# First weights in two transfers, two tiles of x rounded by two engines, and the second tile's products by kind, at the start of a hybrid encoder layer

## The chip, the cores and the metric

The kernel runs on one core of a Trainium2 chip. A core has five engines that run at the same time, each through its own instructions in order: TensorE (PE, the matrix multiplier, with its weight loads, PEld), VectorE (DVE), ScalarE (ACT), GpSimd (POOL) and SyncE (SP, which here only issues transfers). They wait for one another by semaphores. The metric is the device time of one execution, in microseconds (us); lower is better.

## The reference

One layer of an encoder on x of 512 positions by 1024 channels, all in float32:

```
h    = RMSNorm(x) * attn_norm_g
[xr | gate | q | k | v] = h @ w_in                 # 1024 x 2560
y1   = (forward RG-LRU + backward RG-LRU of conv4(xr)) * gelu(gate)
y2   = dilated attention of q, k, v (8 heads, three windows)
x    = x + [RMSNorm(y1) | RMSNorm(y2)] @ w_out
x    = x + relu(RMSNorm(x) @ w_up)^2 @ w_down      # 1024 x 4096 x 1024
out  = RMSNorm(x) * final_norm_g
```

The RG-LRU needs, per channel, a constant softplus(-lam). Only the first line, the first 384 columns of `w_in` and this constant are touched by the change.

## The kernel before

Every large product is made of three matmuls in a rounded float32 type (`FR`): with each operand split into a rounded part `hi` and a remainder `lo`, the product is hi*hi + hi*lo + lo*hi. `mm3` (lines 302 to 305) issues the three for one weight block. The rounding to `hi` is a copy (or a copy with a scale) on ScalarE or DVE, and the remainder `lo` is a subtraction on DVE.

The order of the instructions of TensorE, ScalarE, DVE and GpSimd is the order of the program text; only SP's transfers are put in order by a scheduler, behind what frees their buffers.

The beginning, with the names that matter:

- On TensorE, eight warm-up matmuls of a tile of ones (`pwarm`, line 145) stand ahead of everything. `vt` holds the vectors of gains and constants; ScalarE's queue loads it.
- x comes transposed, in eight tiles of 128 channels by 512 positions, each with the 384 columns of `w_in` that belong to its channels behind it (`xw[k]`, 128 x 896). SP loads them (lines 324 to 327); tile 0 comes in two transfers, x and then weights.
- `cvx(k)` (lines 331 to 341) rounds a tile: `h_hi` is x times the gain, rounded, on ScalarE (333); `w3h` is the rounded weights, on DVE for tile 0 (336) and on ScalarE for the others (338); `h_lo` (339) and `w3l` (340) are the remainders, on DVE.
- `sq(k)` squares x on ScalarE (345), and `addsq` adds the squares up on DVE (348). The sum over tiles gives the RMS of each position. The norm's division comes only after the product, so the matmuls need not wait for it.
- `softplus_consts` (147 to 173) computes the constant of the RG-LRU in pieces, on tiles of 128 x 8: a call of `next(spc)` issues the piece up to the next `yield`. The first piece is two DVE operations (153, 154), the second an exponential on ScalarE (156), the third two DVE operations (158, 159) and the first part of a chain of small GpSimd operations (160 to 167).
- The product of the first 384 columns (lines 405 to 415) adds into three banks `pxr[t]`: nine matmuls a tile. For tile 0 they go by kind: three of h_hi and w3h, three of h_lo and w3h, three of h_hi and w3l. For tiles 1 to 7 each bank has its three in a row (`mm3`). Ahead of tile 7, `col_sums` (402) multiplies the sum of squares, as stationary operand, with a column of ones; then DVE (387), a power on GpSimd (390) and four transposes on TensorE (382) make the row `rrow` by which the products are scaled.

From there on, the weights stream in chunks of 128 x 1024 that `conv_hi` (249 or 251) and `conv_lo` (259) round.

Of the kernel before, what the change touches and what calls it, by code (L numbers as in the profile page):

```python
# [14 lines left out]
AF = mybir.ActivationFunctionType  # L15
OP = mybir.AluOpType

P = 128
S = 512
# [80 lines left out]
def hybrid_kernel(ctx: ExitStack, tc, xw, xn, w_in, w_v, w_out, w_up, w_dn, gates, vecs, rel, onehot, fg, out):  # L100
    nc = tc.nc
# [8 lines left out]
    act = nc.scalar.activation  # L110
# [3 lines left out]
    def g_(name, dt=FT, shape=(P, S)):  # L114
        return work.tile(list(shape), dt, name=name, tag="g", bufs=NG)
# [4 lines left out]
    def ps_(name, tag):  # L120
        return psum.tile([P, S], FT, name=name, tag=tag, bufs={"pj": 4, "gs": 2, "et": 2}[tag])

    def f(t):
        return t.bitcast(FT)
# [5 lines left out]
    def vec(n, i):  # L130
        return vt[:, VEC[n] + i:VEC[n] + i + 1]
# [15 lines left out]
    def softplus_consts():  # L147
        ts, tt = nc.gpsimd.tensor_scalar, nc.gpsimd.tensor_tensor
        lam = vt[:, VEC["lam"]:VEC["lam"] + 8]
        e8, sp, z, z2, pl = [small(n, 8) for n in ("e8", "sp8", "z8", "z28", "pl8")]  # L150
        cneg = consts.tile([P, 8], FT, name="cneg")
        chalf = consts.tile([P, 8], FT, name="chalf")
        stt(e8, lam, -1.0, lam, op0=OP.mult, op1=OP.max)
        nc.vector.tensor_scalar(sp, lam, -1.0, 0.0, op0=OP.mult, op1=OP.max)
        yield
        act(e8, e8, AF.Exp, scale=-1.0)
        yield
        nc.vector.tensor_scalar(z, e8, 2.0, None, op0=OP.add)
        nc.vector.reciprocal(z, z)
        tt(z, z, e8, op=OP.mult)  # L160
        tt(z2, z, z, op=OP.mult)
        ts(pl, z2, 1.0 / 19, 1.0 / 17, op0=OP.mult, op1=OP.add)
        for c in (15, 13, 11, 9, 7, 5, 3, 1):
            if c == 7:
                yield
            tt(pl, pl, z2, op=OP.mult)
            ts(pl, pl, 1.0 / c, None, op0=OP.add)
        tt(pl, pl, z, op=OP.mult)
        ts(pl, pl, 2.0, None, op0=OP.mult)
        tt(sp, pl, sp, op=OP.add)  # L170
        ts(cneg, sp, -LRU_C, None, op0=OP.mult)
        ts(chalf, sp, 0.5 * LRU_C, None, op0=OP.mult)
        yield cneg, chalf

    spc = softplus_consts()
    next(spc)


    chunks = []
# [122 lines left out]
    def mm3(o, a, b, first, last, on=False):  # L302
        nc.tensor.matmul(o, lhsT=a[0], rhs=b[0], start=bool(first), stop=False, skip_group_check=on)  # L303
        nc.tensor.matmul(o, lhsT=a[0], rhs=b[1], start=False, stop=False, skip_group_check=on)  # L304
        nc.tensor.matmul(o, lhsT=a[1], rhs=b[0], start=False, stop=bool(last), skip_group_check=on)  # L305
# [8 lines left out]
    h_hi = big.tile([P, KD, S], FR, name="h_hi", tag="bigA")  # L314
    h_lo = big.tile([P, KD, S], FR, name="h_lo", tag="bigB")
    XW = S + 3 * P
    xwt, w3 = [], []
    for k in range(KD):
        if 4 <= k < 7:
            xwt.append(stream.tile([P, 1024], FT, name="wraw", tag="wraw", bufs=3)[:, :XW])  # L320
        else:
            xwt.append(work.tile([P, 1024], FT, name="tw", tag="tw", bufs=4)[:, :XW])
        if k == 0:
            nc.sync.dma_start(xwt[0][:, :S], xw[0][:, :S])
            nc.sync.dma_start(xwt[0][:, S:], xw[0][:, S:])
        else:
            nc.sync.dma_start(xwt[k], xw[k])

# [1 line left out]

    def cvx(k):
        x, w = xwt[k][:, :S], xwt[k][:, S:]
        act(h_hi[:, k, :], x, AF.Copy, scale=vec("ag", k))
        hi, lo = g_("w3h", FR), g_("w3l", FR)
        if k == 0:
            nc.vector.tensor_copy(hi[:, :3 * P], w)
        else:
            act(hi[:, :3 * P], w, AF.Copy)
        stt(h_lo[:, k, :], x, vec("ag", k), f(h_hi)[:, k, :], op0=OP.mult, op1=OP.subtract)
        nc.vector.tensor_tensor(lo[:, :3 * P], w, f(hi)[:, :3 * P], op=OP.subtract)  # L340
        w3.append((hi, lo))

    def sq(k):
        sqx[k] = g_("sqx")
        act(sqx[k], xwt[k][:, :S], AF.Square)

    def addsq(k):
        nc.vector.tensor_tensor(sqx[0], sqx[0], sqx.pop(k), op=OP.add)

    cvx(0)  # L350
    next(spc)
    sq(0)
    next(spc)
    for k in range(1, KD):
        cvx(k)
        sq(k)
        if k >= 2:
            addsq(k - 1)
# [7 lines left out]
    def hk(k):  # L366
        return (h_hi[:, k, :], h_lo[:, k, :])

    def wk(c, k):
        if c < 3:  # L370
            return tuple(t[:, c * P:(c + 1) * P] for t in w3[k])
        hi, lo = splits[c]
        return (hi[:, k * P:(k + 1) * P], lo[:, k * P:(k + 1) * P])
# [11 lines left out]
    def rstd_cols(ssc, n):  # L385
        v = small("rv", 4)
        nc.vector.tensor_scalar(v, ssc, 1.0 / n, EPS, op0=OP.mult, op1=OP.add)
        r = consts.tile([P, 4], FT, name="rcol_%d" % st["rc"])
        st["rc"] += 1
        nc.gpsimd.tensor_tensor(r, v, mhalf, op=OP.pow)  # L390
        return r
# [7 lines left out]
    def col_sums(ss, tag):  # L399
        pc = ps_("pcs", tag)  # L400
        for tt in range(4):
            nc.tensor.matmul(pc[:, tt:tt + 1], lhsT=ss[:, tt * P:(tt + 1) * P], rhs=ones[:, 0:1], start=True, stop=True)
        return pc[:, 0:4]

    pxr = {t: ps_("pxr", "pj") for t in range(3)}
    for k in range(KD):
        if k == KD - 1:
            rcol = rstd_cols(col_sums(sqx[0], "et"), D)
        if k == 0:
            for i, (a, b) in enumerate(((0, 0), (0, 1), (1, 0))):  # L410
                for t in range(3):
                    nc.tensor.matmul(pxr[t], lhsT=wk(t, 0)[a], rhs=hk(0)[b], start=i == 0, stop=False)
            continue
        for t in range(3):
            mm3(pxr[t], wk(t, k), hk(k), False, k == KD - 1)
# [251 lines left out]
    for n, (k, tt) in enumerate(steps):  # L667
        c = C_V + k // 2
        if k == 0:
            pv[tt] = ps_("pv", vtag[tt])  # L670
        hi, lo = splits[c]
# [433 lines left out]
    for w in OSEQ:  # L1105
        for i in range(4):
            tt, k = (i % 2, i // 2) if w == "s2" else (i // 2, i % 2)
# [239 lines left out]
    for half in range(2):  # L1347
# [5 lines left out]
        start = 0  # L1353
        if half == 0:
            start = 3
# [164 lines left out]
        for j in range(7 * NQ):  # L1520
            _, w, q = seq[j]
# [31 lines left out]
        if half == 1:  # L1553
            b = 6 * NQ
# [75 lines left out]
```

## Time and profile before

| | |
|---|---|
| median of 3 timed runs | 544.73 us (543.91 to 545.04) |
| profiled execution | 544.32 us |
| its span, first to last instruction | 542.5 us |
| PE, DVE, ACT, POOL busy | 533.7, 432.3, 364.0, 63.6 us |
| transfers | 106.96 MB, mean 197 GB/s |

The profile is of one execution. Times are in us from the span's start; a line of the timeline gives start, length, engine, line of the kernel, operation, the tile written and the tiles read, the shapes, a count, and in brackets how long the engine was idle before it and what ended that. Lengths of matmuls are modelled and overlap: the pace is read from the distance of their starts. Successive operations of ScalarE and DVE also overlap a little.

### The profile page before, as it was taken

The numbers are of one execution on the slowest core, as the hardware profiler recorded it, in microseconds if no ns is written. First come the engines' busy times: TensorE is split into PE (matmuls) and PEld (weight loads), VectorE is DVE, ScalarE is ACT, GpSimd is POOL, SyncE is SP. The second block draws the span as 40 slices with busy tenths as digits, with TensorE's granted clock in tenths as the row PEclk, the third lists the DMA queues.
The fourth block names the chain that finished last, engine by engine and source line by source line (L and its number), as shares of the span: only waits on it lengthen the run. The fifth ranks groups of instructions, "written<-read, shape, count | busy, mean of one in ns | idle before, by whom it ended". The sixth has DMA issues, their size and how long they took to land.

```text
span 542.5 us, 8157 instructions
## 1 busy us (share of the span) xinstructions
PE 533.7 (98%) x3018; PEld 453.2 (84%) x3018; DVE 432.3 (80%) x628; ACT 364.0 (67%) x573; POOL 63.6 (12%) x91
## 2 busy tenths in 40 slices
PE   9999999999999999999999999999999999999994
PEld 7856888887887568899999888888999999888883
DVE  6897788996763788889869987879756987886884
ACT  7667973898775744677566855566657686755665
POOL 3330000000001131001030123001001110131000
PEclk9999999999999999999999999999999999999998
DMA  7654275554298787765676699994987496799804
GB/s 273 229 171 140 54 249 179 134 173 147 80 366 205 164 149 201 272 232 146 192 156 170 204 249 275 277 370 108 288 237 201 127 212 184 180 283 261 192 1 156
DMA packets 34360, 106.96 MB, mean 197 GB/s; under 512 B 4228, under 2 KB 5124, under 8 KB 34320
## 3 DMA queue, kind: packets, MB, share of 16 engines
q1 hardware_dynamic: 25600, 76.56, 41.0%
q0 software_dynamic: 7968, 28.76, 28.1%
q10 hardware_dynamic: 752, 1.12, 0.6%
q8 instruction: 24, 0.39, 0.3%
q14 instruction: 16, 0.13, 0.1%
HBM read 98.00 MB, written 4.23 MB: 188 GB/s over the span
## 4 chain that ended last, share of the span: by engine, by line
PE 93%; DVE 3%; ACT 2%; issue 1%; ACTq 0%; DVEq 0%
PE pu L305 10%; PE pu L304 10%; PE pu L303 10%; PE pd L305 8%; PE pd L303 8%; PE pd L304 8%; PE pqk L303 3%; PE pqk L305 3%; PE pqk L304 3%; PE pav L859 3%; PE pt L778 2%; PE pwo L303 2%; PE pwo L305 2%; PE pwo L304 2%; PE pg L489 2%; PE pv L303 1%
## 5 line engine op out<-in xcount | busy, mean ns | idle before, releaser
L259 DVE TENSOR_TENSOR wlo<-wraw,whi 128x1024 fp32r<-128x1024 f32 x73 | 89.0, 1221 | 22.2 <-ACT whi L251 22.0
L251 ACT ACTIVATE whi<-wraw 128x1024 fp32r<-128x1024 f32 x70 | 74.1, 1060 | 38.4 <-PE pd L305 19.6
L303 PE MATMUL pd<-whi,ah 128*128 128x512 f32 x192 | 74.8, 390 | 0.0
L304 PE MATMUL pd<-wlo,ah 128*128 128x512 f32 x192 | 74.8, 390 | 0.0
L305 PE MATMUL pd<-whi,al 128*128 128x512 f32 x192 | 74.8, 389 | 0.0
L304 PE MATMUL pu<-hl,whi 128*128 128x256 f32 x224 | 63.5, 283 | 0.0
L305 PE MATMUL pu<-hh,wlo 128*128 128x256 f32 x224 | 63.5, 283 | 0.0
L303 PE MATMUL pu<-hh,whi 128*128 128x256 f32 x224 | 63.5, 283 | 0.0
L251 ACT ACTIVATE whi<-tw 128x1024 fp32r<-128x1024 f32 x36 | 38.1, 1060 | 33.9 <-PE pu L304 10.0
L305 PE MATMUL pu<-h2h,wlo 128*128 128x256 f32 (+1 forms) x200 | 60.2, 301 | 0.2 <-DVE wlo L259 0.2
L303 PE MATMUL pu<-h2h,whi 128*128 128x256 f32 (+1 forms) x200 | 60.2, 301 | 0.0
L304 PE MATMUL pu<-h2l,whi 128*128 128x256 f32 (+1 forms) x200 | 60.1, 301 | 0.0
L259 DVE TENSOR_TENSOR wlo<-tw,whi 128x1024 fp32r<-128x1024 f32 x36 | 44.0, 1223 | 16.0 <-ACT whi L251 16.0
L251 ACT ACTIVATE whi<-ts 128x1024 fp32r<-128x1024 f32 x24 | 25.5, 1061 | 26.5 <-PE pd L305 18.8
L304 PEld LDWEIGHTS pu<-hl,whi 128*128 128x128 f32 x224 | 43.1, 192 | 0.0
L303 PEld LDWEIGHTS pu<-hh,whi 128*128 128x128 f32 x224 | 43.1, 192 | 0.0
L305 PEld LDWEIGHTS pu<-hh,wlo 128*128 128x128 f32 x224 | 43.1, 192 | 0.0
L305 PEld LDWEIGHTS pd<-whi,al 128*128 128x128 f32 x192 | 36.1, 188 | 7.5
L304 PEld LDWEIGHTS pd<-wlo,ah 128*128 128x128 f32 x192 | 36.1, 188 | 7.5
L303 PEld LDWEIGHTS pd<-whi,ah 128*128 128x128 f32 x192 | 36.1, 188 | 7.3
L305 PEld LDWEIGHTS pu<-h2h,wlo 128*128 128x128 f32 x200 | 38.3, 192 | 1.8 <-DVE wlo L259 0.6
L303 PEld LDWEIGHTS pu<-h2h,whi 128*128 128x128 f32 x200 | 38.3, 192 | 1.3
(261 smaller groups left out, 1262.5 us busy)
## 6 DMA issues: line engine op xcount, KB each, us to landing
wraw<-in_w_up_dram SPq DMA_DIRECT2D x25, 512.0 KB, 3.6
ts<-in_w_dn_dram POOLq DMA_DIRECT2D x24, 512.0 KB, 13.7
wraw<-in_w_dn_dram SPq DMA_DIRECT2D x24, 512.0 KB, 8.8
tw<-in_w_up_dram SPq DMA_DIRECT2D x15, 512.0 KB, 9.4
tw<-in_w_up_dram POOLq DMA_DIRECT2D x15, 512.0 KB, 7.6
wraw<-in_w_in_dram SPq DMA_DIRECT2D x13, 512.0 KB, 3.5
ts<-in_w_dn_dram SPq DMA_DIRECT2D x8, 512.0 KB, 4.6
tw<-in_w_dn_dram SPq DMA_DIRECT2D x8, 512.0 KB, 8.1
```

The costliest lines, as they stand in the source:

```text
L251: act(hi, raws[i], AF.Copy)
L259: nc.vector.tensor_tensor(lo, r, f(splits[i][0]), op=OP.subtract)
L303: nc.tensor.matmul(o, lhsT=a[0], rhs=b[0], start=bool(first), stop=False, skip_group_check=on)
L304: nc.tensor.matmul(o, lhsT=a[0], rhs=b[1], start=False, stop=False, skip_group_check=on)
L305: nc.tensor.matmul(o, lhsT=a[1], rhs=b[0], start=False, stop=bool(last), skip_group_check=on)
L489: nc.tensor.matmul(pg[2 * d + j][halves[b ^ d]], lhsT=gwr[t][halves[b], c], rhs=xc[t][halves[b]], start=True, stop=True)
L778: nc.tensor.transpose(pt[:, qt * P:(qt + 1) * P], en[h][qt][:, jt * P:(jt + 1) * P], ident)
L859: nc.tensor.matmul(pav[p][a, :], lhsT=vs[:, jt, h * DH:(h + 1) * DH], rhs=et.pop((h, jt)), start=jt == 0, stop=jt == 3)
```

## The change

- Tile 0's weights come in two transfers, the first 128 columns and then the other 256.
- For tiles 0 and 1, `h_hi` is written by two engines: in tile 0 ScalarE has the first 256 positions and DVE the other 256, in tile 1 ScalarE has 384 and DVE 128. The weights of both tiles are rounded on DVE, those of tile 0 in two operations (128 and 256 columns), so that tile 1's rounding of weights leaves ScalarE.
- The three first pieces of `softplus_consts` move: from ahead of the loads, behind `cvx(0)` and behind `sq(0)`, to behind `cvx(1)`, `cvx(2)` and `cvx(3)`. DVE then has them behind the remainders of tile 1 (the first piece) and of tile 3 (the third), ScalarE has the exponential behind the weights of tile 2.
- Tile 1's nine matmuls go by kind, as those of tile 0 do.

The number of matmuls stays the same, and so does what is computed. DVE has four operations more (two halves of `h_hi`, the weights of tile 1, and the second part of the weights of tile 0), ScalarE one less, SP one transfer more.

```diff
     spc = softplus_consts()
-    next(spc)
...
         if k == 0:
             nc.sync.dma_start(xwt[0][:, :S], xw[0][:, :S])
-            nc.sync.dma_start(xwt[0][:, S:], xw[0][:, S:])
+            nc.sync.dma_start(xwt[0][:, S:S + P], xw[0][:, S:S + P])
+            nc.sync.dma_start(xwt[0][:, S + P:], xw[0][:, S + P:])
...
     def cvx(k):
         x, w = xwt[k][:, :S], xwt[k][:, S:]
-        act(h_hi[:, k, :], x, AF.Copy, scale=vec("ag", k))
         hi, lo = g_("w3h", FR), g_("w3l", FR)
-        if k == 0:
-            nc.vector.tensor_copy(hi[:, :3 * P], w)
+        if k < 2:
+            c = (S // 2, 3 * P)[k]
+            act(h_hi[:, k, :c], x[:, :c], AF.Copy, scale=vec("ag", k))
+            nc.vector.tensor_scalar(h_hi[:, k, c:], x[:, c:], vec("ag", k), None, op0=OP.mult)
+            for c in ((slice(0, P), slice(P, 3 * P)), (slice(0, 3 * P),))[k]:
+                nc.vector.tensor_copy(hi[:, c], w[:, c])
         else:
+            act(h_hi[:, k, :], x, AF.Copy, scale=vec("ag", k))
             act(hi[:, :3 * P], w, AF.Copy)
...
     cvx(0)
-    next(spc)
     sq(0)
-    next(spc)
     for k in range(1, KD):
         cvx(k)
+        if k < 4:
+            next(spc)
         sq(k)
...
-        if k == 0:
+        if k < 2:
             for i, (a, b) in enumerate(((0, 0), (0, 1), (1, 0))):
                 for t in range(3):
-                    nc.tensor.matmul(pxr[t], lhsT=wk(t, 0)[a], rhs=hk(0)[b], start=i == 0, stop=False)
+                    nc.tensor.matmul(pxr[t], lhsT=wk(t, k)[a], rhs=hk(k)[b], start=i == 0 and k == 0, stop=False)
             continue
```

## The prediction

> **What bounds the kernel now.** I read the page's busy shares and chain first, then busy time by stretches, then the first 21 us instruction by instruction. The page:
>
> ```profile
> PE 533.7 (98%) x3018; PEld 453.2 (84%) x3018; DVE 432.3 (80%) x628; ACT 364.0 (67%) x573; POOL 63.6 (12%) x91
> PE 93%; DVE 3%; ACT 2%; issue 1%; ACTq 0%; DVEq 0%
> ```
>
> TensorE is busy for 98% of the span and carries 93% of the chain that ended last. Stretches (columns: length; busy us and count of PE, PEld, DVE, ACT, POOL; granted clock, DMA share, GB/s):
>
> ```profile
> 4.00:8.00 4.00, 4.00 (x14) 3.33 (x14) 2.84 (x7) 2.80 (x7) 1.39 (x6) 1.00 0.99 351
> 8.00:20.00 12.00, 12.00 (x55) 9.82 (x54) 11.44 (x20) 10.68 (x20) 2.73 (x6) 1.00 0.72 263
> 60.00:540.00 480.00, 474.70 (x2736) 409.39 (x2734) 385.71 (x553) 319.94 (x506) 49.75 (x56) 1.00 0.72 199
> ```
>
> From 4 to 20 us TensorE is never idle, and later it is idle 5.3 of 480 us. So what TensorE gains or loses in its first 20 us is carried to the end almost whole, and the change can be worth only what its first matmuls lose. TensorE's timeline there (start, length, instruction):
>
> ```profile
> 1.04 3.78 PE L145 MATMUL pwarm<-ones 128*128 128x128 f32 x16 [1.04 <-DVE epsb L136]
> 4.20 0.33 PEld L145 LDWEIGHTS pwarm<-ones 128*128 128x128 f32 x1
> 4.54 0.29 PEld L412 LDWEIGHTS pxr<-h_hi,w3h 128*128 128x128 f32 x1
> 4.57 1.62 PE L412 MATMUL pxr<-h_hi,w3h 128*128 128x512 f32 x3
> 5.99 1.40 PE L412 MATMUL pxr<-h_lo,w3h 128*128 128x512 f32 x3
> 7.23 0.86 PE L412 MATMUL pxr<-h_hi,w3l 128*128 128x512 f32 x3
> 7.92 0.39 PE L303 MATMUL pxr<-h_hi,w3h 128*128 128x512 f32 x1
> 8.15 0.40 PE L304 MATMUL pxr<-h_lo,w3h 128*128 128x512 f32 x1
> 8.30 0.19 PEld L305 LDWEIGHTS pxr<-h_hi,w3l 128*128 128x128 f32 x1 [0.19 <-DVE w3l L340]
> ```
>
> Two things are to be seen. The warm-up matmuls fill TensorE until the first real one: their sixteen weight loads come every 0.21 us (1.04 to 4.20), so a next load was due at 4.41, and the real one came at 4.54, 0.13 us late. And the pace changes inside tile 0: three matmuls in 1.42 us and three in 1.24 us, then three in 0.69 us and 0.23 us each from there on. TensorE ran at half pace until about 7.2 us. That is not a wait for data: while it runs slowly, tile 1 gets ready behind it. The granted clock in the stretch from 4 to 8 us reads 1.00 and doesn't show this.
>
> **The change part by part.** The profiled execution took 544.32 us (span 542.5 and 1.82 around it); the median of the three timed runs is 544.73, 0.41 higher. I sum against the profiled execution and add the result to the median.
>
> The engines that feed TensorE:
>
> ```profile
> 3.73 0.17 DVE L153 SCALAR_TENSOR_TENSOR e<-vt 128x8 f32<-128x8 f32 x1 [2.73 <-DMA vt<-in_vecs_dram]
> 4.06 0.36 DVE L336 CAST w3h<-tw 128x384 fp32r<-128x384 f32 x1
> 4.48 0.75 DVE L339 SCALAR_TENSOR_TENSOR h_lo<-tw,vt,h_hi 128x512 fp32r<-128x512 f32 x1
> 5.15 0.55 DVE L340 TENSOR_TENSOR w3l<-tw,w3h 128x384 fp32r<-128x384 f32 x1
> 5.62 0.16 DVE L158 TENSOR_SCALAR z<-e 128x8 f32<-128x8 f32 x1
> 5.82 0.20 DVE L159 RECIPROCAL z<-z 128x8 f32<-128x8 f32 x1
> 7.02 0.76 DVE L339 SCALAR_TENSOR_TENSOR h_lo<-tw,vt,h_hi 128x512 fp32r<-128x512 f32 x1 [1.00 <-ACT h_hi L333]
> 7.70 0.55 DVE L340 TENSOR_TENSOR w3l<-tw,w3h 128x384 fp32r<-128x384 f32 x1
> 8.57 0.75 DVE L339 SCALAR_TENSOR_TENSOR h_lo<-tw,vt,h_hi 128x512 fp32r<-128x512 f32 x1 [0.32 <-ACT h_hi L333]
> 10.33 0.74 DVE L339 SCALAR_TENSOR_TENSOR h_lo<-tw,vt,h_hi 128x512 fp32r<-128x512 f32 x1
> 18.40 1.47 DVE L348 TENSOR_TENSOR sqx<-sqx 128x512 f32<-128x512 f32 x2
> 3.73 0.72 ACT L333 ACTIVATE h_hi<-tw,vt 128x512 fp32r<-128x512 f32 x1 [1.06 <-DMA vt<-in_vecs_dram]
> 6.27 0.72 ACT L333 ACTIVATE h_hi<-tw,vt 128x512 fp32r<-128x512 f32 x1 [1.20 <-DMA tw<-in_xw_dram]
> 6.89 0.51 ACT L338 ACTIVATE w3h<-tw 128x384 fp32r<-128x384 f32 x1
> 7.31 0.61 ACT L345 ACTIVATE sqx<-tw 128x512 f32<-128x512 f32 x1
> 7.83 0.71 ACT L333 ACTIVATE h_hi<-tw,vt 128x512 fp32r<-128x512 f32 x1
> ```
>
> *First weights in two transfers.* The queue and one transfer:
>
> ```profile
> 1.17 0.42 SPq L325 DMA_DIRECT2D tw<-in_xw_dram  x1
> 1.64 1.37 SPq L327 DMA_DIRECT2D tw<-in_xw_dram  x3
> tw<-in_xw_dram SPq DMA_DIRECT2D x1, 192.0 KB, 2.9
> ```
>
> One issue more costs SP 0.47 us (1.17 to 1.64) and moves the seven later tiles' issues by as much. The weights landed at 1.17 + 2.9 = 4.07, just when the cast began, so they, not DVE, set that start. The first third may land from 3.73 (when the vectors had landed) to 4.07, the rest from 4.07 to 4.54 (4.07 + 0.47). For tile 1, which landed at 6.27, the delay is between 0 and 0.47 us; the transfer engines were 0.99 busy from 4 to 8 us, so they have a backlog and the issue is hidden behind it: I take 0 to 0.1. The transfers of tiles 5 and 6 now wait for older ones to land (tile 6's alone did); they are used after 12 us, and an uncovered issue would cost the same 0.47.
>
> *Tile 0 in two halves.* Prices (groups by form: line, engine, shapes, count, busy, mean ns):
>
> ```profile
> L249 DVE CAST whi<-wraw 128x1024 fp32r<-128x1024 f32 x3 | 2.1, 685 | 0.0
> L1193 DVE SCALAR_TENSOR_TENSOR hsum<-hm,hsum 128x256 f32<-128x256 f32 x4 | 1.7, 424 | 0.1
> L817 ACT ACTIVATE oh<-osum 128x256 fp32r<-128x256 f32 x8 | 3.1, 416 | 2.2 <-DVE osum L840 2.2
> ```
>
> DVE casts of 384 and 1024 columns take 0.361 and 0.685 us, 0.506 ns a column: 0.30 for 256 and 0.23 for 128. DVE's half of h_hi costs 0.30 if it runs like a cast, 0.42 if like the 128x256 scalar_tensor_tensor; I take 0.30, since it has one source as the cast has. ScalarE's half costs 0.42 at least (the 128x256 row) and 0.50 at most (0.72 less 256 columns at the 0.83 ns between the 512 and 384 columns, 0.61 and 0.51 us). From 3.73, h_hi is ready at 4.23 instead of 4.45. DVE then casts the first third until 4.30 to 4.38 and the rest until 4.6 to 4.85. An engine sees another's end 0.09 us later (4.45 to the load at 4.54), so the first weight load comes at 4.41 to 4.47, a gain of 0.07 to 0.13, but it can't come before 4.41 because the warm-up matmuls are still there. The second load, due about 4.8, may wait for the rest of the cast until 4.94. Both ends are matmuls at half pace, worth half once the pace doubles at a fixed time: between -0.06 and +0.07 us. I take -0.03.
>
> *Tile 1.* Its h_hi is shared 384:128, its w3h cast goes from ScalarE (0.51) to DVE (0.36). With the same landing: ScalarE 6.27 to 6.89 at the most; DVE 0.23 + 0.36 until about 6.8; h_lo from 6.96 instead of 7.02, w3l done at 8.18 instead of 8.25. TensorE reaches tile 1 only at 7.92, when three of the four operands lie ready; the fourth delayed one load until 8.30, some 0.02 us of matmul pace. Going by kind puts the first w3l matmul 0.68 us into the tile, where it can't be late. Gain: 0.02. What hides the rest is tile 0 at half pace; without that cover the earlier operands would count (the first rival).
>
> *The small constants.* Their DVE operations left two idle places: e and sp stood while the first weights were on their way, z and its reciprocal while tile 1 was. They now stand after tile 1 and after tile 3. From 8.57 on DVE has no idle place: h_lo, w3l and the sum of squares of a tile take 1.74 us, a round against TensorE's 2.05. The start of h_lo of tile 2 is set by ScalarE: two operations instead of three for tile 1, so its h_hi may start at 7.31 if x has landed, else up to 7.83; h_lo starts between 8.25 (behind e and sp) and 8.57, I take 8.4. The reciprocal pair adds 0.36. The sums of squares ended at 18.40 + 1.47 = 19.87; they now end at 19.87 - 0.17 + 0.36 = 20.06, between 19.91 and 20.23. Who waits:
>
> ```profile
> 19.99 1.08 PEld L402 LDWEIGHTS pcs<-ones,sqx 128*128 128x128 f32 x8
> 10.55 0.61 POOL L167 TENSOR_SCALAR pl<-pl 128x8 f32<-128x8 f32 x1
> 21.44 1.96 POOL L390 TENSOR_TENSOR rcol<-rv,mhalf 128x4 f32<-128x4 f32 x1 [10.28 <-DVE rv L387]
> ```
>
> TensorE loads that sum as weights at 19.99, in order, ahead of tile 7. It had 0.12 us to spare; with 0.09 us of signal it will get it at 20.15 (20.00 to 20.32). So whatever TensorE wins before, it waits here: +0.16 against before, between 0.01 and 0.33. GpSimd's chain stands behind that reciprocal, which ended at 6.02 and will end near 11.6; so the chain ends near 16.7 instead of 11.16 (10.55 + 0.61); its power operation starts at 21.44, 4.7 us later, so that is free, and without this cover it would cost its delay one for one. The exponential moves on ScalarE, which runs ahead of DVE by then.
>
> Sum: the gains in tiles 0 and 1 (0.05) end in the wait for the sum of squares and are not added to it: +0.16 - 0 = about +0.1 us after rounding, 544.4 for such an execution and 544.8 against the median. A measurement of this kernel can tell about 0.2%, 1.1 us, from no change; this is far inside.
>
> The Trainium skill, "TensorE: Matmul & The Clock Gate", Part 1, says that the array starts at half clock and opens after a busy window of about 3.4 us that runs free of the kernel's start. The trace agrees so far as the pace doubles once, 6.2 us after the first matmul; if the phase is free, other executions open sooner or later than 7.2.
>
> **The rivals.** *Pace up early, and the sums in time.* If TensorE reaches full pace soon after 4.6, tile 0 ends near 6.8 and before waits for tile 1: h_hi and w3h at 7.40, h_lo at 7.78, w3l at 8.25, tile end 9.97 (8.39 and seven paces of 0.23), as late as in this execution. After the change: kind one from 6.96, kind two from 7.78, kind three to 9.1. That is 0.8 us, and 1.3 (half of 4.57 to 7.2) is all that could ever be had. It needs the sums of squares 0.8 us sooner than I reckon, that is tile 2's landing and DVE's operations at their cheapest. Time 543.4 to 544.2. For it: these are the operands that the change makes early. Against it: the 19.87.
>
> *Pace up late (slower).* If the weights' second part lands so late (past 4.9) that TensorE stands still between warm-up and tile 0, and that break makes it begin its 6.2 us anew, full pace comes at 11.0 instead of 7.2: 3.8 us at half pace, 1.9 us lost, 546.6. By the Trainium skill's window in the same section it would be 3.4 us, 1.7 lost, by its estimate 546.4. Against it: the break of 0.13 us in this execution did not stop the pace from rising.
>
> *Tile 1 late by the whole 0.47 us.* Then ScalarE, DVE's row and the sums go with it: 0.47 more at the sums, less what ScalarE had in hand, 545.2 to 545.4. Against it: the backlog of transfers.
>
> **How the numbers follow.** Forecast 0.58, early pace 0.22, late pace 0.10, late tile 0.10. More than 0.2% faster means below 543.64: something over half of the early case and the scatter of the runs, 0.14. More than 0.2% slower means above 545.82: the late pace and a little scatter, 0.11. The rest, 0.75, lies within. The range runs from 543.6 to 545.9, which leaves out most of the late pace and half of the early one; the likeliest case's own is 544.2 to 545.4.
>
> **What would show it.** Right: the first real weight load at 4.41 to 4.5; tile 1's operands ready before TensorE gets there; a wait of TensorE for the sum of squares just ahead of tile 7, near 20.1; SP's tile 1 issue near 2.1 with the landing still near 6.3. Wrong: a TensorE that passes that sum well before 19.8 without waiting; a break in TensorE between 4.6 and 7 with half pace after 8 us; a landing of tile 1 past 6.6.

## The result and the profile after

The changed kernel takes 546.05 us (median of 8 runs, 545.59 to 546.8), the kernel before 544.63 us beside it (8 runs). The ratio is 1.0026, with a 95% interval of 1.0017 to 1.0034: slower by 0.9 to 1.9 us. The forecast was no change that can be measured. The profiled execution took 546.8 us with a span of 544.9 us, 0.75 above the median; that of before had a span of 542.5.

The page of the changed kernel (busy shares, then the chain's shares by engine):

```profile
PE 533.8 (98%) x3018; PEld 451.9 (83%) x3018; DVE 432.9 (79%) x632; ACT 363.3 (67%) x572; POOL 65.3 (12%) x91
PE 86%; DVE 5%; DMA 5%; ACT 2%; issue 1%; SPq 0%; ACTq 0%; DVEq 0%
```

TensorE's work is the same, 533.8 us against 533.7; the loss is idle time. Transfers, which had no share in the chain before, now carry 5% of it, 4 of these 5 points at the second place below. The stretches (columns as in the prediction) say where:

```profile
4.00:8.00 4.00, 3.34 (x13) 2.15 (x12) 2.00 (x6) 1.12 (x3) 0.00 (x0) 1.00 0.89 307
8.00:20.00 12.00, 11.74 (x52) 9.37 (x51) 11.87 (x26) 11.41 (x22) 5.51 (x11) 1.00 0.69 255
180.00:190.00 10.00, 8.91 (x53) 6.39 (x50) 7.20 (x15) 9.56 (x19) 0.88 (x1) 1.00 0.67 126
```

TensorE was never idle from 4 to 20 us before; now it is idle 0.66 and 0.26 us there. A second place, between 180 and 190 us, costs 1.1 us. The start, on TensorE, DVE and SP (timelines of the changed kernel):

```profile
4.54 0.73 PE L416 MATMUL pxr<-h_hi,w3h 128*128 128x512 f32 x1
5.94 0.73 PE L416 MATMUL pxr<-h_hi,w3h 128*128 128x512 f32 x2 [0.66 <-DVE w3h L339]
8.52 0.93 PE L416 MATMUL pxr<-h_hi,w3h 128*128 128x512 f32 x3 [0.26 <-ACT h_hi L336]
10.77 0.39 PE L302 MATMUL pxr<-h_hi,w3h 128*128 128x512 f32 x1
21.39 1.05 PE L406 MATMUL pcs<-ones,sqx 128*128 128x1 f32 x8 [0.24 <-DVE sqx L352]
3.91 0.35 DVE L337 TENSOR_SCALAR h_hi<-tw,vt 128x256 fp32r<-128x256 f32 x1 [2.91 <-DMA vt<-in_vecs_dram]
4.17 0.22 DVE L339 CAST w3h<-tw 128x128 fp32r<-128x128 f32 x1
5.59 0.29 DVE L339 CAST w3h<-tw 128x256 fp32r<-128x256 f32 x1 [1.20 <-DMA tw<-in_xw_dram]
7.82 0.28 DVE L337 TENSOR_SCALAR h_hi<-tw,vt 128x128 fp32r<-128x128 f32 x1 [0.80 <-DMA tw<-in_xw_dram]
1.64 0.42 SPq L325 DMA_DIRECT2D tw<-in_xw_dram  x1
2.10 1.39 SPq L327 DMA_DIRECT2D tw<-in_xw_dram  x3
tw<-in_xw_dram SPq DMA_DIRECT2D x1, 128.0 KB, 3.9
```

The engines' prices came out near what was expected: the halves of h_hi take 0.35 us on DVE and 0.51 on ScalarE, the casts 0.22 and 0.29. What is late is the data. The weights' second part, issued at 1.64, took 3.9 us and landed at 5.54, where the whole had landed at 4.07; one real matmul runs and then TensorE stands. Tile 1, issued 0.46 us later, landed 1.55 us later, 7.82 for 6.27. The rates of the transfer engines from 0 to 12 us (GB/s in 40 slices of 0.3 us), before and then after:

```profile
GB/s 0 0 0 0 0 34 160 57 342 389 382 420 364 323 382 311 203 335 394 335 311 323 394 418 382 382 406 430 382 406 394 442 418 406 418 394 454 430 335 215
```

```profile
GB/s 0 0 0 0 0 34 137 180 308 333 306 214 118 65 106 137 249 321 299 335 346 382 394 418 370 418 394 382 418 418 430 406 418 418 394 430 442 394 394 430
```

Before, the rate stays above 300 from 2.4 to 4.8 us. After, it falls to between 65 and 137 from 3.6 to 4.8 us. Taken together, that stretch in the two kernels (the last two columns are the busy share of the transfer engines, which adds up packet times and can pass 1, and GB/s; before, then after):

```profile
3.60:4.80 1.20, 1.20 (x7) 1.19 (x7) 0.93 (x4) 1.07 (x3) 0.00 (x0) 1.00 1.02 345
```

```profile
3.60:4.80 1.20, 1.20 (x7) 1.20 (x6) 0.49 (x2) 0.90 (x2) 0.00 (x0) 1.00 0.61 106
```

So the backlog on which the prediction counted is not there in the changed kernel. Nor is it that tile 1's issue came too late to fill the engines: its first packets (3.5 KB each) start at 3.33 us before and at 3.46 after, but between 3.6 and 4.8 us 115 of them start before and 25 after (counted in the traces).

The second place, in the changed kernel: ScalarE in its order waits for an accumulating transfer of w_out, and what stands behind it on ScalarE (`ett`) makes TensorE wait.

```profile
180.44 1.06 ACT L250 ACTIVATE whi<-ws 128x1024 fp32r<-128x1024 f32 x1 [7.26 <-DMA ws<-in_w_out_dram]
PE prow L386 <- ACT ett L784: 1.1, 1, 1.1
```

### The profile page after: what moved, and what is told of

Same layout as the page of the kernel before. It is cut to its first block, busy times and chain, and to the rows that moved or that the text cites. A ratio compares the mean times of both kernels' runs of the same rounds, so it can differ in the third digit from the quotient of the medians.

```text
span 544.9 us, 8161 instructions
## 1 busy us (share of the span) xinstructions
PE 533.8 (98%) x3018; PEld 451.9 (83%) x3018; DVE 432.9 (79%) x632; ACT 363.3 (67%) x572; POOL 65.3 (12%) x91
## 4 chain that ended last, share of the span: by engine, by line
PE 86%; DVE 5%; DMA 5%; ACT 2%; issue 1%; SPq 0%; ACTq 0%; DVEq 0%
PE pu L304 10%; PE pu L303 10%; PE pu L302 10%; PE pd L302 8%; PE pd L303 8%; PE pd L304 8%; DMA ws<-in_w_out_dram 4%; PE pqk L302 3%; PE pqk L304 3%; PE pqk L303 3%; PE pt L782 2%; PE pwo L302 2%; PE pwo L304 2%; PE pwo L303 2%; PE pg L493 2%; PE pv L302 1%
## 5 line engine op out<-in xcount | busy, mean ns | idle before, releaser
L258 DVE TENSOR_TENSOR wlo<-ts,whi 128x1024 fp32r<-128x1024 f32 x24 | 29.3, 1221 | 12.8 <-ACT whi L250 12.7
```

What stands on the lines that cost most here:

```text
L258: nc.vector.tensor_tensor(lo, r, f(splits[i][0]), op=OP.subtract)
```

## The experiments

Two questions: which part of the change costs, and by what.

**The change without the split.**

```diff
-            nc.sync.dma_start(xwt[0][:, S:S + P], xw[0][:, S:S + P])
-            nc.sync.dma_start(xwt[0][:, S + P:], xw[0][:, S + P:])
+            nc.sync.dma_start(xwt[0][:, S:], xw[0][:, S:])
```

> All of the change except the split of tile 0's weights: they come in one transfer again, as before. Theory A (the extra transfer makes the weights' second part and tile 1 land late): tile 1 lands near 6.3 us instead of 7.8, no wait of TensorE between its first and second real matmul, and the time goes back to 544.3 to 545.0. Theory B (the rounding by two engines and the moved constants load DVE so that TensorE waits for the sum of squares): a wait ahead of tile 7 stays, and the time stays near 546.

544.66 us, ratio 0.9992 (0.9979 to 1.0005). Tile 1 is taken up at 6.92, 0.6 later than expected though 0.9 earlier than in the changed kernel, TensorE has no break at the weights, and a wait of 0.25 us for the sum of squares ahead of tile 7 stays. The loss is gone: theory A. The wait that B names is there, a quarter of a microsecond long.

**The split alone, in the kernel before** (the same lines the other way).

> The kernel before with nothing but tile 0's weights in two transfers. Theory A: the weights' second part lands near 5.5 us and tile 1 near 7.8, TensorE stands still for a microsecond inside tiles 0 and 1, time 545.5 to 546.3. Theory B: no difference from before, 544.3 to 545.0.

546.66 us, ratio 1.0033 (1.0019 to 1.0046). The split alone costs as much as the whole change or more. TensorE's waits (total, times, longest), and where ScalarE takes up tile 1:

```profile
PE pxr L413 <- DVE w3h L337: 1.3, 1, 1.3
PE pxr L303 <- ACT w3h L339: 1.1, 1, 1.1
8.29 0.72 ACT L334 ACTIVATE h_hi<-tw,vt 128x512 fp32r<-128x512 f32 x1 [3.09 <-DMA tw<-in_xw_dram]
```

**Both kernels once more.**

> The changed kernel once more, unchanged, for a second profiled execution. If the late landings at the start are a property of the kernel, tile 1 lands near 7.8 us again and TensorE waits near 5 and near 8; if they were an accident of one execution, near 6.3. The wait of 1.1 us near 181 us, for a transfer of w_out, is open: both theories allow that it comes or doesn't.

546.0 us, ratio 1.0019 (1.0010 to 1.0029). The late landings are there again: the second cast starts at 5.00, tile 1 at 7.53. The wait near 181 us is not, and the span is 543.5 instead of 544.9: that second place is an accident of single executions (it was seen in 4 of the 15 profiled ones of all kernels, in none of the 3 of the kernel before, with 8 or 12 warm-up matmuls; so few can't say whether the change makes it likelier).

> The kernel before once more, for a second profiled execution: tile 1 near 6.3 us and the pace of the matmuls doubling at another time than 7.2 us if that time is free of the kernel's start. Time 544.6.

545.15 us, ratio 1.0003 (0.9993 to 1.0013). In this execution the pace was already full at the first real matmul, and tile 1 came at 6.93, behind a milder dip of the rate (108 to 251 GB/s from 4.5 to 6.0 us). So TensorE waits for tile 1 where it did not in the first profile:

```profile
4.65 0.94 PE L412 MATMUL pxr<-h_hi,w3h 128*128 128x512 f32 x3
8.11 0.50 PE L303 MATMUL pxr<-h_hi,w3h 128*128 128x512 f32 x1 [1.13 <-ACT w3h L338]
```

**What makes the transfers late: the short rows, or one transfer more?** First the same split by partitions, with rows of 1.5 KB:

```diff
-            nc.sync.dma_start(xwt[0][:, S:], xw[0][:, S:])
+            nc.sync.dma_start(xwt[0][:64, S:], xw[0][:64, S:])
+            nc.sync.dma_start(xwt[0][64:, S:], xw[0][64:, S:])
```

> The kernel before with tile 0's weights in two transfers cut the other way: partitions 0 to 63 and 64 to 127, all 384 columns, so each row stays 1.5 KB long. Theory A1 (what costs is one issue more on SP ahead of tile 1): tile 1 lands at 7.5 to 8.3 us as with the split by columns, 546 to 546.7. Theory A2 (what costs is the short rows of 0.5 and 1 KB): tile 1 lands 0.5 us later than before at most, near 6.8 to 7.3, 544.9 to 545.5.

546.7 us, ratio 1.0030 (1.0019 to 1.0042): as slow with long rows, so A2 falls. The ten runs lie in two groups, four from 544.75 to 545.5 and six from 546.56 to 547.28, and the profiled one (545.1) is of the first: the weights' second half came at 5.79 but tile 1 at 6.73, so the two needn't be late together. What the second group lost is in no profile. The dip of the rate, though, is in this one too: 126 GB/s from 3.6 to 4.8 us.

A tiny third transfer, in the kernel before:

```diff
-            nc.sync.dma_start(xwt[0][:, S:], xw[0][:, S:])
+            nc.sync.dma_start(xwt[0][:, S:S + 376], xw[0][:, S:S + 376])
+            nc.sync.dma_start(xwt[0][:, S + 376:], xw[0][:, S + 376:])
```

> The kernel before with 376 of tile 0's weight columns in the second transfer and the last 8 columns (4 KB) in a third. If one transfer more ahead of tile 1 costs by itself, whatever it carries, the cast of the weights waits for the tiny third transfer until 5.0 to 5.8 us and tile 1 lands at 6.7 to 8.3: 545.5 to 546.7. If it is the bytes of the second part that come late, the tiny one lands by 4.6 and the time is 544.7 to 545.3.

546.01 us, ratio 1.0025 (1.0013 to 1.0037). A third transfer of four kilobytes costs as much as the larger one did. DVE in this kernel, and TensorE behind it:

```profile
5.26 0.36 DVE L337 CAST w3h<-tw 128x384 fp32r<-128x384 f32 x1 [1.20 <-DMA tw<-in_xw_dram]
5.77 1.62 PE L413 MATMUL pxr<-h_hi,w3h 128*128 128x512 f32 x3 [0.94 <-DVE w3h L337]
7.18 1.48 PE L413 MATMUL pxr<-h_lo,w3h 128*128 128x512 f32 x3
9.74 0.42 PE L303 MATMUL pxr<-h_hi,w3h 128*128 128x512 f32 x1
```

The tiny transfer was issued at 1.64 and used at 5.26, 3.6 us later. Here the pace stayed at half until 9.74, so tile 0 took 4 us from 5.77. Tile 1 came at 7.01, hardly later than in the kernel before (6.93 in its second profile): in this execution the loss at the start comes from the late weights.

The second part on another queue, in the changed kernel:

```diff
     nc.scalar.dma_start(vt, vecs)
+    nc.scalar.dma_start(x0t[:, S + P:], xw[0][:, S + P:])
...
-            nc.sync.dma_start(xwt[0][:, S + P:], xw[0][:, S + P:])
```

> The changed kernel, with the second part of tile 0's weights issued from ScalarE's queue right behind the vectors, so that SP's issue of tile 1 is back at 1.64 us; the rows are as short as in the changed kernel. Theory A1: tile 1 lands at 6.3 to 6.9 us again, 544.2 to 544.8. Theory A2: it stays late, 545.6 to 546.2.

544.4 us, ratio 0.9998 (0.9989 to 1.0007). With the same rows and as many transfers in all, but SP's issue of tile 1 back at 1.64 (and the second part's own issue at 1.17), the loss is gone: tile 1 at 6.70, no break inside tile 0, and 312 GB/s from 3.6 to 4.8 us. What costs is the third issue ahead of tile 1 in SP's row. The rate in that stretch says the same for all fifteen profiles: 94 to 132 GB/s in the six with three such issues, whatever these carry, and 294 to 416 in the nine with one or two.

One issue less, in the kernel before:

```diff
-            nc.sync.dma_start(xwt[0][:, :S], xw[0][:, :S])
-            nc.sync.dma_start(xwt[0][:, S:], xw[0][:, S:])
+            nc.sync.dma_start(xwt[0], xw[0])
```

> The kernel before with tile 0, x and weights, in one transfer: one issue less, tile 1's at 1.17 us. Theory A1: the landing of tile 1 follows the issue the other way too, near 5.3 to 5.8 us, and TensorE doesn't wait for it; tile 0 itself lands near 4.1 instead of 3.8, so 544.2 to 544.8. Theory A2: tile 1 lands as before, 6.3 to 6.9.

543.95 us, ratio 0.9992 (0.9982 to 1.0001). Tile 1 follows the other way too: ScalarE takes it at 5.71 without a wait, the rate never falls below 330 once it is up, and TensorE doesn't wait for it. Tile 0 is taken at 4.46 instead of 3.73.

**The small constants back in their place, without the split.**

```diff
     spc = softplus_consts()
+    next(spc)
...
     cvx(0)
+    next(spc)
     sq(0)
+    next(spc)
     for k in range(1, KD):
         cvx(k)
-        if k < 4:
-            next(spc)
```

> The change without the split and with the pieces of the small constants where they were before (two engines' rounding and the order by kind stay). If the moved constants cost, as the prediction had it, the 0.3 us that TensorE waits for the sum of squares ahead of tile 7 in the change without the split shrinks to nothing, and the time falls from 544.66 to about 544.3. If they cost nothing, the wait stays and the time is 544.6 to 544.8.

544.1 us, ratio 0.9988 (0.9979 to 0.9998). TensorE passes the sum of squares at 20.05 with no idle time of note, though the squares still end last, at 19.99. Against the same with moved constants (tile 1 at 6.92, sum at 20.48) the distance from tile 1 to the sum shrinks from 13.56 to 13.43 us; most of the 0.43 is the earlier tile. The intervals of the two kernels overlap. This is the one kernel whose interval against the kernel before lies below 1, and narrowly: one of a dozen may do so by chance.

**Looking for a better one.** Tile 0's weights whole on ScalarE's queue, constants in place, two engines' rounding:

> The change without the split, with the constants back in their place, and tile 0's weights issued whole from ScalarE's queue behind the vectors, so that SP's issue of tile 1 comes at 1.17 us. If the place in SP's row of issues is what sets tile 1's landing, it lands near 5.7 us as it did with tile 0 in one transfer, while tile 0's x and weights land by 4.2; TensorE then has no wait in tiles 0 and 1, and the time is 543.3 to 544.0. If the two queues share what makes the transfers late, tile 1 stays at 6.3 to 6.9 and the time at 544.1 to 544.7.

546.06 us, ratio 1.0020 (1.0009 to 1.0031): a miss. Tile 1 came at 5.28 as hoped, but the weights, second on ScalarE's queue beside SP's tile 1, came at 5.46. There is no dip here (406 GB/s from 3.6 to 4.8 us): the packets of the weights and of tile 1 move side by side. TensorE stood for 1.01 us behind the warm-up and then ran at half pace until about 10, as it did until 9.74 with the tiny transfer.

The same rounding with tile 0 in one transfer:

> The same two engines' rounding, order by kind and constants in place, with tile 0 in one transfer on SP. Tile 0 lands near 4.4 and tile 1 by 5.7: against the kernel before with tile 0 in one transfer (543.95) the earlier operands of tile 1 can no longer gain, since TensorE did not wait for tile 1 there; tile 0's two halves gain up to 0.2. So 543.5 to 544.0. If the two engines' rounding were worth something by itself, it would be below 543.4.

544.46 us, ratio 0.9996 (0.9988 to 1.0005), above what was expected. The profiled execution passed the sum of squares at 19.65, the earliest of all, and then lost 1.4 us at the place near 181 us. The gain at the start doesn't show in the median; how often the accident there eats it, a handful of profiles can't say.

**Does the break in TensorE cost by itself?** The warm-up of 12 matmuls instead of 8, in both kernels:

```diff
-    for _ in range(8):
+    for _ in range(12):
```

> The changed kernel with 12 warm-up matmuls instead of 8, which keep TensorE busy to about 6.3 us at half pace (four more at 0.43 us), past the late landing of tile 0's weights. Theory C (a good part of the loss is that the break in TensorE near 5 us keeps the pace at half for longer): no break is left, the pace doubles by 8 us in the profile, and the time falls to 545.0 to 545.6. Theory D (the loss is the late operands alone, of tile 0 and above all of tile 1): the time stays at 545.8 to 546.6.

545.77 us, ratio 1.0011 (1.0001 to 1.0020), between what C and D expected. No break is left at the weights, tile 1 comes at 8.18, and TensorE passes the sum of squares at 21.74, waiting 0.27 us for it: 13.56 us behind tile 1, as in the changed kernel with its break. So the trace speaks for D, and the time alone doesn't decide.

> The kernel before with 12 warm-up matmuls: the control. The first real matmul moves from 4.6 to about 6.3 us while nothing is late. By itself this costs at most what tile 0 then lacks before tile 1 is ready: tile 0 at full pace takes 2.1 us, to 8.4, and tile 1 was waited for until 7.9 to 8.1, so 0.3 to 0.5 us more, 545.0 to 545.3; if half pace lasts past 7 us in most executions, up to 545.8.

544.79 us, ratio 1.0002 (0.9988 to 1.0015): a later first matmul, at 5.58, costs the kernel before nothing, less than expected. In this kernel TensorE's early matmuls are not what sets the end; tile 1 is.

## Why the prediction was wrong

One table carries it. For the profiled executions: when ScalarE takes up tile 1, when TensorE takes the sum of squares, their distance, the span beyond that, what TensorE lost near 181 us (from its waits), and when the full clock begins. This last is the start of the first stretch in the trace's own record of the granted clock. It falls where the distance of the matmuls' starts halves (from 0.43 to 0.23 us at 512 columns); ahead of it nothing is recorded, and the stretches shown above read 1.00 there all the same.

| kernel | tile 1 | sum | distance | span less sum | near 181 | full clock |
|---|---|---|---|---|---|---|
| before | 6.27 | 20.21 | 13.94 | 522.3 | - | 7.17 |
| before again | 6.93 | 20.91 | 13.98 | 522.2 | - | 4.67 |
| before, 12 warm-ups | 6.75 | 20.71 | 13.96 | 522.1 | - | 4.92 |
| split alone | 8.29 | 22.24 | 13.95 | 522.4 | - | 4.61 |
| split by partitions | 6.73 | 20.72 | 13.99 | 522.4 | - | 4.24 |
| changed | 7.82 | 21.39 | 13.57 | 523.5 | 1.1 | 5.11 |
| changed again | 7.53 | 21.09 | 13.56 | 522.4 | - | 5.04 |
| changed, 12 warm-ups | 8.18 | 21.74 | 13.56 | 522.5 | - | 7.24 |
| changed, no split | 6.92 | 20.48 | 13.56 | 522.2 | - | 5.24 |
| changed, second part on ScalarE's queue | 6.70 | 20.25 | 13.55 | 522.3 | - | 3.98 |
| changed, no split, constants back | 6.62 | 20.05 | 13.43 | 522.4 | - | 4.97 |
| tiny third transfer | 7.01 | 22.05 | 15.04 | 523.0 | 0.6 | 9.76 |
| weights on ScalarE's queue | 5.28 | 22.18 | 16.90 | 523.0 | - | 9.99 |
| before, tile 0 in one | 5.71 | 20.29 | 14.58 | 522.9 | 0.8 | 6.57 |
| two engines' rounding, tile 0 in one | 5.37 | 19.65 | 14.28 | 523.8 | 1.4 | 4.50 |

Behind the sum of squares every kernel takes 522.1 to 522.5 us, beside the accident near 181 (with the weights on ScalarE's queue 0.5 us more, which TensorE lost waiting for a remainder of the weights, `wlo`, later on). And up to it, in the first ten rows, the distance from the landing of tile 1 is fixed by the kind of kernel: 13.94 to 13.99 with the rounding of before, 13.55 to 13.57 with that of the changed kernel. (The last four rows are the exceptions: with the tiny transfer and with the weights on ScalarE's queue the half pace, not tile 1, sets the sum, and with tile 0 in one transfer tile 1 lies ready before TensorE is through with tile 0.) So the change gave 0.4 us for a given landing and moved the landing from 6.27, 6.93 and 6.75 (mean 6.65) to 7.82, 7.53 and 8.18 (mean 7.84): 1.19 less 0.4 is 0.8 us. The timed difference is 1.4 us (0.9 to 1.9) and in the second comparison 1.0 (0.5 to 1.6). The 0.8 is from three executions of each, one of them with 12 warm-up matmuls; what more there is, whether the accident near 181, rarer late landings or, in some executions, a late full clock, stays open.

Step by step:

- *The transfer engines "have a backlog and the issue is hidden behind it: I take 0 to 0.1".* This is the step that failed. Tile 1 came 1.19 us later on average. The 0.99 busy from 4 to 8 us, on which the step rested, is a mean of the kernel before; it was taken to hold with one transfer more in the row. It does not hold: from 3.6 to 4.8 us the engines were busy 1.02 of the time at 345 GB/s before, and 0.61 at 106 after. Even the upper bound, the 0.47 us of the issue, was too low, and the weights' rest came at 5.0 to 6.0 with the split, not at 4.54 at the latest. That bound took a transfer's time to landing (2.9) as fixed, from the one row there was; the rest, in third place, took 3.3 to 4.4 us in the three profiles of the changed kernel. Why the transfers crawl behind one issue more stays open.
- *The rivals.* "Tile 1 late by the whole 0.47" was the right mechanism at less than half its size, and had 0.10. "Pace up late" is what the tiny transfer and the weights on ScalarE's queue show: TensorE stood for 0.94 and 1.01 us before the full clock had come, and it then came at 9.76 and 9.99, 4.0 and 4.2 us behind the first matmul after the break, not 6.2. But in both profiles of the changed kernel the full clock began at 5.11 and 5.04 us, so it is not their cause. Where it had come first, breaks of 1.3 and 1.7 us (the split alone, the split by partitions) did not bring the half pace back.
- *The first weight load at 4.41 to 4.5.* It came at 4.51, with h_hi begun at 3.91 instead of 3.73 because the vectors landed later. Right that the warm-up leaves no room there.
- *Tile 1's rounding gains 0.02, since TensorE reaches it only at 7.92.* True of that execution alone. In the second profile of before TensorE was at full pace earlier and stood before tile 1 for 1.1 us, and for a given landing of tile 1 the changed kernel is 0.4 us sooner at the sum. So the earlier operands and the order by kind together are worth 0.4 us: the rival "pace up early, and the sums in time" in half its size.
- *The wait for the sum of squares ahead of tile 7, near 20.1.* It is there in each kernel with moved constants, 0.22 to 0.27 us, and no longer shown when they are put back; it hid part of the gain as said. That the constants cost 0.36 was too much: the distance from tile 1 grows by 0.13, in one execution. (The sum itself, +0.16, was rounded to 0.1; as it stood it gives 544.9 and not 544.8.)
- *GpSimd's chain is free.* It ends at 19.56 and not near 16.7, since its operations ran longer here (0.34 to 0.61 us, and it began at 13.18), but still before the power operation at 22.73.

On the free phase of the pace, as "TensorE: Matmul & The Clock Gate" of the Trainium skill has it in Part 1, the traces agree: in two executions of the kernel before, the full clock began at 7.17 and at 4.67 us.

## What to carry to other kernels

A first transfer split in two made the rest of the weights late in each of the six profiles and tile 1 late in four of them (7.53 to 8.29), while in the changed kernel the first weight load came only 0.03 us sooner (4.51 for 4.54). At the start of a kernel, count the issues that stand ahead of each tile, and ask which landing the end follows (here tile 1's, at a fixed distance) before the first tile's is improved. A busy share of the transfer engines, read before the change, does not prove that a backlog stays when one more transfer is put into the row: here 1.02 at 345 GB/s became 0.61 at 106. And take a second profiled execution of the kernel before, if one is to be had, before something is called hidden: here the work that hid tile 1 in the first was not there in the next.

## What the runs showed of the hardware

- A transfer of 4 KB in the third place of SP's row, with tile 1 behind it, was used 3.6 us after its issue; in the kernel before, 192 KB in second place took 2.9 to 3.0. One issue takes SP 0.47 us, but one more of them ahead of tile 1 moved its landing by 1.2 us on average in the changed kernel, and in six of six profiles it brought the rate from 3.6 to 4.8 us down to 94 to 132 GB/s. On ScalarE's queue, issued at 1.17, 128 KB landed in time to be rounded by 4.56 us, while 192 KB there, beside tile 1 on SP's, came at 5.46. Why the third transfer slows the row was not settled: the rows' length is excluded (the dip is there with rows of 1.5 KB), and the bytes are too (4 KB).
- TensorE's full clock began anywhere from 3.98 to 9.99 us, and at 7.17 and 4.67 in two executions of one kernel. A break of about 1 us ahead of it went with the two latest starts; breaks of 1.3 and 1.7 us behind it left the pace full. The granted clock in the profile's stretches reads 1.00 in the half-paced part too, since nothing is recorded there; the start of the record shows the change.
